# Raw weight blocks in one ring of six, and two of four weight sums made by accumulating DMAs

## The chip, the cores and the metric

The kernel runs on one core of a Trainium2 chip. The metric is the device time of one execution in microseconds; of several executions the median counts. The engines are named as in the profile: PE (matrix products; PEld its weight loads), DVE (elementwise work on two operands), ACT (activations and copies), POOL (small elementwise work, and DMAs of its own), SP (issues most of the DMAs). Each engine takes its instructions in order.

## The reference

One decoder block on x of 1024 tokens by 1024 columns, all in float32:

```python
proj = x @ w_in                     # 1024 x 7168: q | f | i | og | pool_v | gate_a | gate_b
a = HGRN2(q, f, i)                  # 8 heads, state recurrence in chunks
a = per-head RMSNorm(a) * g * sigmoid(og) @ w_a
b = per-group linear(causal_mean_w(pool_v) - pool_v) * pool_scale   # 4 groups, windows 2, 4, 8, 16
mix = (sigmoid(gate_a) * a + sigmoid(gate_b) * b) @ w_out
x = LN(alpha * x + mix)
x = LN(alpha * x + relu(x @ w_up)^2 @ w_down)      # w_up 1024 x 4096
```

## The kernel before

**Products.** Each float32 operand is split into two parts of a shorter type (`split`, L115 to L120: ACT copies the high part, L118, DVE subtracts for the low part, L119), and a product is the sum of three matmuls (`prod`, L201, L203, L204). The large products follow the Winograd form of Strassen's scheme: of an operand's four blocks, seven products instead of eight are made, from blocks and sums of blocks. On the side of the tokens the operands are a11, a12, a22 and the sums s1 to s4. They stay in SBUF, split, for a whole stage.

**A pair.** `pair` takes two column blocks of a weight, 128 columns each. Both have an upper and a lower half of 512 rows: b11 and b21 are the first column block, b12 and b22 the second. Seven operands are made from them (`t0` is b11, `b_21`, `t3`, `t2`, `t1`, `t4`, `b_22`), each split into two tiles of the ring "w" of ten, and seven products `p1` to `p7` of twelve matmuls each are added into three PSUM banks (a, c, z). ACT copies a bank (L271) where its sum so far is needed, DVE adds (L275). The four sums of weight blocks are DVE instructions: L241 (`w_diff`, twice), L284 and L289, or L291 and L292 in a "twin" pair. In a pair that is no twin, t3 and t2 are made together and then p6 and p7 run; then t1 and t4, then p5 and p4. In a twin (the pairs of w_a, and the first two of w_up) the order is p7, p4, p6, p5, each with its operand.

**Raw weights.** A pair has two raw tiles, one for each half of the rows; each holds two blocks of 256 KB. `raw_tile` is a ring of two, so one pair fills it. SP issues the loads: L217 where the two column blocks are neighbours (one DMA of 512 KB for each tile), L223 where they aren't (four of 256 KB). The sums go to a ring "t" of two tiles.

**Stages in order.** The values (v = x @ their part of w_in), the heads, the gates and pools, the product with w_a, that with w_out and the first norm, the up products with w_up, the down products with w_down and the last norm. In the heads stage the pairs of the next head (`head_inputs`), the output gates (every second head) and the pools stand beside the recurrence `hgrn` of the current head, whose small factors are made by POOL (L819 to L838). After the last head come the gates, the pool products and the sums of o (`EXTRAS[7, 1]`, `o_sums` L608 to L613). The up stage runs sixteen pairs, the first three interleaved, the others one after the other.

**Order of work.** The program is written stage by stage, and a planner orders the instructions of each engine by priorities and its own model of their times: an instruction whose operands are ready passes one that still has to wait. The order is then fixed. DMAs are issued by an engine in that order too, and an issue that waits for a buffer holds what is behind it on the same engine.

Of the kernel before, what the change touches and what calls it, by code (L numbers as in the profile page):

```python
# [43 lines left out]
def tile_hybrid_block(  # L44
# [126 lines left out]

    def first_tokens(name, *tags):
        for kp in range(CH):
            ps, _ = transposed(r[:CH], HALF if name == "a12" else 0, kp, tags[kp % len(tags)])
            in_parts(name, kp, ps)
            A.copy(xt[name == "a12"][kp], ps)

    def second_tokens(name, *tags):
        a11, a12, s = xt
        turned = []  # L180
        for kp in range(CH):
            if name in ("s3", "a22"):
                ps, done = transposed(r[CH:], HALF if name == "a22" else 0, kp, tags[kp % len(tags)])
                turned.append(done)
            if name == "s3":
                V.tensor_sub(s[kp], a11[kp], ps)
            elif name == "s1":
                V.tensor_add(a11[kp], s[kp], a11[kp])
            elif name == "s4":
                V.tensor_sub(a12[kp], a12[kp], s[kp])  # L190
            in_parts(name, kp, dict(s3=s, s2=s, s1=a11, s4=a12)[name][kp] if name != "a22" else ps)
            if name == "a22":
                V.tensor_sub(s[kp], ps, s[kp])
        return turned
# [11 lines left out]
    def raw_tile():  # L206
        return wq.tile([P, CH, 2, P], F32, tag="raw", name=nm("raw"), bufs=2)

    def w_blocks(src, c1, c2, tile_of=raw_tile):

        raw = tile_of(), tile_of()

        def load(*which):
            for kh in range(2):
                rows_of = src[kh * HALF : (kh + 1) * HALF, :].rearrange("(k p) c -> p k c", p=P)
                if c2 == c1 + P and len(which) == 2:
                    done = nc.sync.dma_start(  # L217
                        out=raw[kh].rearrange("p k n c -> p k (n c)"), in_=rows_of[:, :, c1 : c1 + 2 * P]
                    )
                else:  # L220
                    for n in which:
                        c = (c1, c2)[n]
                        done = nc.sync.dma_start(out=raw[kh][:, :, n], in_=rows_of[:, :, c : c + P])  # L223
            return done

        return raw, load

    def loaded_blocks(*args):
        raw, load = w_blocks(*args)
        load(0, 1)  # L230
        return raw
# [6 lines left out]

    def w_diff(a, b):
        t = wq.tile([P, CH, P], F32, tag="t", name=nm("t"), bufs=2)  # L240
        V.tensor_sub(t, a, b)  # L241
        return t
# [20 lines left out]
    def pair(raw, rooms, takes, pz_tag="pj", twin=False, pc_tag="pj"):  # L263


        b11, b12, b21, b22 = raw if len(raw) == 4 else (raw[kh][:, :, n] for kh in range(2) for n in range(2))
        c, ps = {}, {}
# [10 lines left out]
        def t3():  # L278
            c["t"] = w_diff(b22, b12)
            return w_part(c["t"])  # L280

        def t2():
            if not twin:
                V.tensor_add(c["t"], c["t"], b11)  # L284
            return w_part(c["t"])

        def t4():
            if not twin:
                V.tensor_sub(c["t"], b21, c["t"])  # L289
                return w_part(c["t"])  # L290
            V.tensor_add(c["t"], c["t"], b11)  # L291
            V.tensor_sub(b21, b21, c["t"])  # L292
            return w_part(b21)

        def t1():
            return w_part(w_diff(b12, b11))
# [17 lines left out]
        def p6(w):  # L314
            prod(ps["a"], w, "s2", False)
            with tc.high_priority(PRIO):
                c[21] = copied(rooms[1], ps["a"])
                if twin:
                    takes[2](added(c[21], ps["z"]))

        def p4(w):
            prod(ps["z"], w, "a22", False)
            if not twin:
                with tc.high_priority(PRIO):
                    takes[2](added(c[21], ps["z"]))
# [17 lines left out]
        def b_22():  # L343
            return w_part(b22)

        return (
            ((t0,), ((t0, p1),)),
            ((b_21,), ((b_21, p2),)),
            *(
                (((t3,), ((t3, p7),)), ((t4,), ((t4, p4),)), ((t2,), ((t2, p6),)), ((t1,), ((t1, p5),)))  # L350
                if twin
                else (((t3, t2), ((t2, p6), (t3, p7))), ((t1, t4), ((t1, p5), (t4, p4))))
            ),
            ((b_22,), ((b_22, p3),)),
# [47 lines left out]
    with tc.tile_pool(name="xr", bufs=8, side="right", reuse_waits="tile") as xr:  # L402
# [42 lines left out]
        def raw_tile_rows():  # L445
            return [raw_tile().rearrange("p k n c -> p (k n c)").rearrange("p (k c) -> p k c", c=HALF) for _ in range(2)]
# [78 lines left out]
        def take_p5(c, ps):  # L525
            V.tensor_add(c22[c], c22[c], ps)
            put(1, 1, c, c22[c])

        def take_p3(c, ps):
            t = c_soon()  # L530
            A.copy(t, ps)
            put(0, 1, c, t)
# [9 lines left out]
        with behind_parts("a12"):  # L542
            for k in range(CH):
                V.tensor_sub(b22[k], b22[k], b12[k])
            w = parts(b22)
# [3 lines left out]
        with behind_parts("s3"):  # L549
            for k in range(CH):  # L550
                V.tensor_add(b22[k], b22[k], b11[k])
                V.tensor_sub(b21[k], b21[k], b22[k])
            w = parts(b21)
# [7 lines left out]
        with tc.issue_after(taken["a22", 1]):  # L561
            for k in range(CH):
                V.tensor_sub(b12[k], b12[k], b11[k])
# [21 lines left out]
    def raw_rows(src, k2, cc):  # L585

        raw = raw_tile().rearrange("p k n c -> p (k n c)").rearrange("p (k c) -> p k c", c=HALF)
        rows_of = src[k2 * P : (k2 + 2) * P, cc * HALF : (cc + 1) * HALF].rearrange("(k p) c -> p k c", p=P)
        nc.sync.dma_start(out=raw, in_=rows_of)
# [15 lines left out]
    def o_sums(kp, tile_of=c_tile):  # L605

        a11, a21, a12, a22 = (loaded(od[k][u], tile_of) for k, u in ((kp, 0), (kp, 1), (kp + CH, 0), (kp + CH, 1)))
        V.tensor_add(a22, a21, a22)  # L608
        V.tensor_sub(a21, a11, a21)
        V.tensor_sub(a11, a22, a11)  # L610
        V.tensor_sub(a12, a12, a11)
# [6 lines left out]
    with tc.tile_pool(name="tmp", bufs=1, side="right", reuse_waits="tile") as tmp:  # L618
# [24 lines left out]
        def head_inputs(h, behind=()):  # L643
# [6 lines left out]
            def take_f(u):  # L650
                def take(src):
                    t = fs[u] = fs[u] or tt("f")
                    A.activation(t, src, AF.Sigmoid)
# [3 lines left out]
            def take_q(u):  # L657
# [7 lines left out]
                loaded_blocks(w_in, h * P, D + h * P), (c_soon, c_late, room_f),  # L665
# [8 lines left out]
        def output_gates(h):  # L674

            def take(dst, src=False):
                def put(t):
                    s = c_late() if src else t
                    A.activation(s, t, AF.Sigmoid)
# [4 lines left out]
                loaded_blocks(w_in, 3 * D + h * P, 3 * D + (h + 1) * P), (c_soon, c_late, c_late),  # L684
                (take(ogd[h][0]), take(ogd[h + 1][0], True), take(ogd[h][1]), take(ogd[h + 1][1])),
            ))

        def gates(j):
# [3 lines left out]
            def take(dst, src=None, more=None):  # L692
                def put(t):
                    s = (tt("v") if spare else c_late()) if src else t
                    more_of = loaded(more, lambda: tt("v")) if more is not None else None
                    A.activation(s, t, AF.Sigmoid)
# [7 lines left out]
                loaded_blocks(w_in, 5 * D + j * P, 6 * D + j * P), rooms,  # L704
                (take(gad[j][0]), take(gbd[j][0], True, more[0]), take(gad[j][1]), take(gbd[j][1], False, more[1])),
            ))

        def pool_products(g):
# [6 lines left out]
            raw = raw_tile().rearrange("p k n c -> p (k n c)")[:, : 2 * 2 * P].rearrange("p (k c) -> p k c", c=2 * P)  # L715
# [16 lines left out]
        def pooled(g):  # L732
# [3 lines left out]
            def mean(c, u):  # L736

                for lo in (QUARTER, 0):
# [8 lines left out]
                    if u == 0 and lo == 0:  # L747
                        n += win - 1
                        V.tensor_mul(cur[:, HALO:n], cur[:, HALO:n], inv_n[:, : win - 1])
                        V.tensor_sub(pv[:, HALO:n], cur[:, HALO:n], pv[:, HALO:n])  # L750
                    V.scalar_tensor_tensor(pv[:, n:], cur[:, n:], 1.0 / win, pv[:, n:], ALU.mult, ALU.subtract)
# [11 lines left out]
            def first(c, i):  # L763
                G.memset(c[:, :HALO], 0.0)
                mean(c, 0)
                put(c, i, 0)

            def second(c, i):
                mean(c, 1)
# [12 lines left out]
            def take_12(ps):  # L782
# [7 lines left out]
                loaded_blocks(w_in, 4 * D + j * P, 4 * D + (j + 1) * P),  # L790
# [154 lines left out]
        nxt = head_inputs(0, (None, None, "p6", None, None))  # L945
# [40 lines left out]
        def gated(j, u, park):  # L986

            def take(src):
                t = loaded(gad[j][u], mg_tile("ga", 12))
                V.tensor_mul(t, t, src)  # L990
# [10 lines left out]
        def a_pair(p):  # L1001
            raw = loaded_blocks(w_a, 2 * p * P, (2 * p + 1) * P, raw_tile if p % 2 else mg_raw)
            room = mg_tile("room", 4)
            takes = [gated(2 * p + i, u, p < 2) for u in range(2) for i in range(2)]
            return pair(raw, (c_tile, room, room), takes, "hg", True)
# [76 lines left out]
    with tc.tile_pool(name="wo", bufs=1, side="right", reuse_waits="tile") as mp:  # L1082
        st1 = [None] * 8
        g1, b1 = ln_params(lambda: f(act_tile()).rearrange("p a b -> p (a b)"), ln1_g, ln1_b)
        for k2 in range(0, KT, 2):
            raw = raw_rows(w_out, k2, 1)
            for k in range(2):
                n = len(wo)
                out_row(raw[:, k], (
# [46 lines left out]
    with tc.tile_pool(name="up", bufs=1, side="right", reuse_waits="tile") as up:  # L1136
# [10 lines left out]
        def relu2(t, src):  # L1147
            A.activation(t, src, AF.Relu)
# [3 lines left out]
        def units(i, raw):  # L1152
# [5 lines left out]
            def take(n):  # L1158
                def take(src):
                    h[n] = relu2(c_tile() if n == 1 else src, src)  # L1160
# [20 lines left out]
            return pair(raw, (c_tile,) * 3, (take(0), last, take(2), take(3)), "hg", i < 2, "tr" if i == 2 else "pj")  # L1181

        def up_blocks(i):
            return w_blocks(w_up, i * 2 * P, i * 2 * P + P, up_raw_tile if i % 2 else raw_tile)

        blocks = [up_blocks(i) for i in range(2)]
        for _, load in blocks:
            load(0, 1)
        pairs = [units(i, raw) for i, (raw, _) in enumerate(blocks)]
# [21 lines left out]
        for i in range(3, NP):  # L1211
            raw, load = up_blocks(i)
            w_load = load(0, 1)
            if i == NP - 2:
                for part in down_rows(0, ws0):
                    part(w_load)
# [185 lines left out]
```

## Time and profile before

| | |
|---|---|
| median of 3 runs | 1461.98 us (1461.56 to 1463.47) |
| the profiled execution | 1460.19 us |
| its span, first to last instruction | 1458.5 us |
| granted clock, mean | 0.996 |
| PE, DVE, ACT, POOL busy | 98%, 78%, 52%, 4% |
| moved by DMA | 226.82 MB, 156 GB/s over the span |

The profile is one execution; times in it are counted from its first instruction. An engine is busy while an instruction of its own runs. Matmuls overlap, so the number of matmuls in a stretch says more of PE's pace than the duration of one. "A <- B" in a list of waits means that A stood idle until B released it.

### The profile page before, as it was taken

How to read it: one execution, taken by the hardware profiler on the slowest of the kernel's cores; microseconds unless marked ns; L12 is line 12 of the kernel's file. 1: busy time of each engine (PE TensorE's matmuls, PEld its weight loads, DVE VectorE, ACT ScalarE, POOL GpSimd, SP SyncE). 2: the span in 40 equal slices, each digit the busy share in tenths (PEclk: the TensorE clock that was granted, in tenths of full speed). 3: DMA queues.
4: the chain of work that ended last, by engine and by line, in shares of the span. 5: the costliest groups of instructions: out<-in, count | busy, mean ns of one | idle time of the engine just before them, and what ended most of it. 6: DMA issues, size and time to landing. Idle time of an engine off the chain costs nothing.

```text
span 1458.5 us, 20662 instructions
## 1 busy us (share of the span) xinstructions
PE 1436.4 (98%) x7377; PEld 1187.9 (81%) x7377; DVE 1141.6 (78%) x1838; ACT 758.3 (52%) x1383; POOL 58.6 (4%) x244
## 2 busy tenths in 40 slices
PE   8999999999999998999999999999999999999997
PEld 7888888888888886788888878888888888888886
DVE  5967989899898885768985597666666787777977
ACT  5445565666656655556542376555555443333535
POOL 0001001001000010000002100000000100000000
PEclk9999999999999999999999999999999999999999
DMA  7232233323234447897672225444474874445322
GB/s 253 70 126 87 85 98 101 109 75 114 90 99 138 152 132 249 301 299 241 223 247 99 73 94 195 159 146 144 152 261 149 275 260 150 153 141 163 130 73 116
DMA packets 160615, 226.82 MB, mean 156 GB/s; under 512 B 11232, under 2 KB 84480, under 8 KB 160512
## 3 DMA queue, kind: packets, MB, share of 16 engines
q1 hardware_dynamic: 158576, 218.93, 44.7%
q0 software_dynamic: 1152, 4.19, 0.8%
q10 hardware_dynamic: 784, 2.38, 0.5%
q8 instruction: 58, 0.95, 0.3%
q14 instruction: 45, 0.37, 0.1%
HBM read 154.16 MB, written 71.30 MB: 155 GB/s over the span
## 4 chain that ended last, share of the span: by engine, by line
PE 94%; DVE 3%; DMA 1%; ACT 1%; issue 0%; SPq 0%; DVEq 0%
PE ps_pj L201 16%; PE ps_pj L203 16%; PE ps_pj L204 16%; PE ps_pj L1283 4%; PE ps_pj L1285 4%; PE ps_pj L1284 4%; PE ps_pj L106 3%; PE ps_pj L107 3%; PE ps_pj L105 2%; PE ps_tr L1285 1%; PE ps_tr L1283 1%; PE ps_tr L1284 1%; PE ps_sc L201 1%; PE ps_sc L203 1%; PE ps_sc L204 1%; PE ps_hg L203 1%
## 5 line engine op out<-in xcount | busy, mean ns | idle before, releaser
L201 PE MATMUL ps_pj<-act,w 128*128 128x512 f32 x1068 | 421.6, 395 | 0.4 <-ACT act L123 0.2
L203 PE MATMUL ps_pj<-act,w 128*128 128x512 f32 x1068 | 415.1, 390 | 0.5 <-DVE act L124 0.5
L204 PE MATMUL ps_pj<-act,w 128*128 128x512 f32 x1068 | 414.1, 390 | 0.0
L201 PEld LDWEIGHTS ps_pj<-act,w 128*128 128x128 f32 x1068 | 200.6, 188 | 42.8 <-ACT act L123 0.6
L204 PEld LDWEIGHTS ps_pj<-act,w 128*128 128x128 f32 x1068 | 200.5, 188 | 42.3
L203 PEld LDWEIGHTS ps_pj<-act,w 128*128 128x128 f32 x1068 | 200.6, 188 | 40.6 <-DVE act L124 0.9
L118 ACT CAST w<-t 128x512 fp32r<-128x512 f32 x170 | 104.7, 620 | 105.0 <-PE ps_pj L203 53.8
L118 ACT CAST w<-raw 128x512 fp32r<-128x512 f32 x143 | 88.2, 620 | 117.3 <-PE ps_pj L203 62.5
L119 DVE TENSOR_TENSOR w<-raw,w 128x512 fp32r<-128x512 f32 x143 | 99.8, 702 | 55.2 <-ACT w L118 53.9
L119 DVE TENSOR_TENSOR w<-t,w 128x512 fp32r<-128x512 f32 x170 | 115.9, 685 | 29.6 <-ACT w L118 29.4
L1245 ACT CAST act<-act 128x1024 fp32r<-128x1024 f32 x66 | 66.9, 1050 | 107.9 <-issue 35.0
L1246 DVE TENSOR_TENSOR act<-act,act 128x1024 fp32r<-128x1024 f32 x66 | 79.3, 1220 | 18.5 <-ACT act L1245 15.8
L1285 PE MATMUL ps_pj<-act,act 128*128 128x512 f32 x240 | 92.9, 389 | 0.0
L1284 PE MATMUL ps_pj<-act,act 128*128 128x512 f32 x240 | 92.9, 389 | 0.0
L1283 PE MATMUL ps_pj<-act,act 128*128 128x512 f32 x240 | 92.4, 389 | 0.0
L275 DVE TENSOR_TENSOR c<-c,ps_pj 128x512 f32<-128x512 f32 x95 | 64.5, 681 | 18.0 <-PE ps_pj L204 13.4
L271 ACT COPY c<-ps_pj 128x512 f32<-128x512 f32 x96 | 55.2, 582 | 12.8 <-PE ps_pj L204 12.8
L817 DVE RECIPROCAL tC<-tA 128x128 f32<-128x128 f32 x64 | 54.1, 904 | 0.0
L1284 PEld LDWEIGHTS ps_pj<-act,act 128*128 128x128 f32 x240 | 45.1, 188 | 9.4
L1285 PEld LDWEIGHTS ps_pj<-act,act 128*128 128x128 f32 x240 | 45.1, 188 | 9.4
L1283 PEld LDWEIGHTS ps_pj<-act,act 128*128 128x128 f32 x240 | 45.1, 188 | 9.3
L241 DVE TENSOR_TENSOR t<-raw,raw 128x512 f32<-128x512 f32 x43 | 29.6, 689 | 21.9 <-DMA raw<-in_w_in_dram 19.7
(415 smaller groups left out, 2719.8 us busy)
## 6 DMA issues: line engine op xcount, KB each, us to landing
h<-c SPq DMA_DIRECT2D x106, 256.0 KB, 2.1
act<-h SPq DMA_DIRECT2D x78, 256.0 KB, 2.9
raw<-in_w_in_dram SPq DMA_DIRECT2D x64, 256.0 KB, 3.4
draw<-in_w_down_dram SPq DMA_DIRECT2D x16, 1024.0 KB, 7.8
raw<-in_w_up_dram SPq DMA_DIRECT2D x30, 512.0 KB, 4.2
raw<-in_w_in_dram SPq DMA_DIRECT2D x18, 512.0 KB, 4.0
hf<-h SPq DMA_DIRECT2D x34, 256.0 KB, 2.9
c<-o SPq DMA_DIRECT2D x24, 256.0 KB, 3.4
```

Source lines behind the costliest of these rows:

```text
L118: A.copy(hi, src)
L119: V.tensor_sub(lo, src, f(hi))
L201: PE.matmul(ps, wh[:, k], th, start=first and k == 0, stop=False, skip_group_check=True)
L203: PE.matmul(ps, wh[:, k], tl, start=False, stop=False, skip_group_check=True)
L204: PE.matmul(ps, wl[:, k], th, start=False, stop=k == CH - 1, skip_group_check=True)
L271: A.copy(t, ps)
L275: V.tensor_add(t, t, ps)
L1245: A.copy(hi, src)
L1246: V.tensor_sub(lo, src, f(hi))
L1283: PE.matmul(ps, hh[:, w], wh, start=fresh and n == 0, stop=False, skip_group_check=True)
L1284: PE.matmul(ps, hh[:, w], wl, start=False, stop=False, skip_group_check=True)
L1285: PE.matmul(ps, hl[:, w], wh, start=False, stop=n == M - 1, skip_group_check=True)
```

## The change

- All raw blocks are tiles of their own, [128, 4, 128], in one ring of six (`block_tile`) in place of the two rings "raw" and "t". A pair uses five of them: four blocks and one for a sum. Other users of the raw ring take one to four such tiles. Pairs 1 and 3 of w_a and all pairs of w_up from the fourth on, with the first, now load single blocks of 256 KB (`loaded_blocks`); pairs 0 and 2 of w_a and the second of w_up keep wide loads in rings of their own (`wide_blocks`).
- In the heads, the output gates, the gates and the pools (`summed_blocks`), the sums b22 + b12 and b11 + b12 are made by loading one block with SP and adding the other onto it with an accumulating DMA from POOL (`accum_op=ALU.add`). DVE makes the other two sums. Elsewhere DVE makes all four.
- So that all sums of weight blocks are additions, b12 and b21 stand with the other sign in the scheme. The sums of token blocks change with them (`minus_sum`), and where a result comes out negative its sign is taken back at its use (a scale of -1 in an activation, a sign in `gated`, the other operation in the pools).
- Every pair now runs in the order t0 p1, b_21 p2, t3 p7, t4 p4, t2 p6, t1 p5, b_22 p3, each operand with its product.

```diff
+    def minus_sum(out, a, b):
+        V.scalar_tensor_tensor(out, a, -1.0, b, ALU.mult, ALU.subtract)
...
-    def raw_tile():
-        return wq.tile([P, CH, 2, P], F32, tag="raw", name=nm("raw"), bufs=2)
...
+    def block_tile(shape=(CH, P)):
+        return wq.tile([P, *shape], F32, tag="raw", name=nm("raw"), bufs=6)
+
+    def wide_block(src, kh, c, t):
+
+        rows_of = src[kh * HALF : (kh + 1) * HALF, :].rearrange("(k p) c -> p k c", p=P)
+        done = nc.sync.dma_start(out=t, in_=rows_of[:, :, c : c + t.shape[2]])
+        return t, done
+
+    def loaded_blocks(src, c1, c2, done=None):
+
+        raw = {}
+        for i in ((0, 0), (1, 0), (0, 1), "t", (1, 1)):
+            raw[i] = block_tile(), None
+            if i != "t":
+                raw[i] = wide_block(src, i[0], (c1, c2)[i[1]], raw[i][0])
+        if done is not None:
+            done.append(raw[1, 1][1])
+        return [raw[i][0] for i in ((0, 0), (0, 1), (1, 0), (1, 1), "t")]
+
+    class Summed(tuple):
+        pass
+
+    def summed_blocks(src, c1, c2):
+
+        def load(t, kh, n, onto=False):
+            rows_of = src[kh * HALF : (kh + 1) * HALF, :].rearrange("(k p) c -> p k c", p=P)
+            rows_of = rows_of[:, :, (c1, c2)[n] : (c1, c2)[n] + P]
+            if onto:
+                nc.gpsimd.dma_start(out=t, in_=rows_of, accum_op=ALU.add)
+            else:
+                nc.sync.dma_start(out=t, in_=rows_of)
+
+        b11, b21, t3, t1, b22 = (block_tile() for _ in range(5))
+        load(b11, 0, 0)
+        load(b21, 1, 0)
+        load(t3, 1, 1)
+        load(t3, 0, 1, True)
+        load(t1, 0, 0)
+        load(t1, 0, 1, True)
+        load(b22, 1, 1)
+        return Summed((b11, t1, b21, b22, t3))
...
         def t3():
-            c["t"] = w_diff(b22, b12)
+            if not summed:
+                c["t"] = block_tile() if t is None else t
+                V.tensor_add(c["t"], b22, b12)
             return w_part(c["t"])
 
+        def t4():
+            if not summed:
+                V.tensor_add(b12, b12, b11)
+            V.tensor_add(c["t"], b22, b12)
+            V.tensor_add(b21, b21, c["t"])
+            return w_part(b21)
+
         def t2():
-            if not twin:
-                V.tensor_add(c["t"], c["t"], b11)
             return w_part(c["t"])
...
         def t1():
-            return w_part(w_diff(b12, b11))
+            return w_part(b12)
...
+        return tuple(
+            ((operand,), ((operand, product),))
+            for operand, product in ((t0, p1), (b_21, p2), (t3, p7), (t4, p4), (t2, p6), (t1, p5), (b_22, p3))
         )
...
             run(pair(
-                loaded_blocks(w_in, h * P, D + h * P), (c_soon, c_late, room_f),
+                summed_blocks(w_in, h * P, D + h * P), (c_soon, c_late, room_f),
...
-        def relu2(t, src):
-            A.activation(t, src, AF.Relu)
+        def relu2(t, src, n):
+            A.activation(t, src, AF.Relu, scale=-1.0 if n % 2 else 1.0)
...
-            raw, load = up_blocks(i)
-            w_load = load(0, 1)
+            done = []
+            raw = loaded_blocks(w_up, i * 2 * P, i * 2 * P + P, done)
```

151 lines of the change are left out of this document (57 added, 94 removed).

## The prediction

> **What bounds the kernel now.** I read the page's parts 1 and 4 first, then the stretches, the waits, and the timeline where the one gap stands.
>
> ```profile
> span 1458.5 us, 20662 instructions
> PE 1436.4 (98%) x7377; PEld 1187.9 (81%) x7377; DVE 1141.6 (78%) x1838; ACT 758.3 (52%) x1383; POOL 58.6 (4%) x244
> PE 94%; DVE 3%; DMA 1%; ACT 1%; issue 0%; SPq 0%; DVEq 0%
> ```
> ```profile
> 300.00:350.00 50.00, 50.00 (x348) 41.72 (x347) 48.96 (x100) 33.24 (x76) 4.50 (x26) 1.00 0.30 95
> 550.00:600.00 50.00, 43.25 (x252) 34.83 (x252) 28.76 (x52) 24.34 (x57) 0.00 (x0) 0.93 0.77 254
> 600.00:650.00 50.00, 50.00 (x221) 40.96 (x220) 31.91 (x50) 25.79 (x44) 0.00 (x0) 1.00 0.95 315
> 1000.00:1050.00 50.00, 50.00 (x222) 41.44 (x221) 29.25 (x45) 26.72 (x45) 0.00 (x0) 1.00 0.45 148
> ```
>
> A stretch shows its length, then busy PE, PEld, DVE, ACT, POOL, the granted clock, the DMA share and GB/s. TensorE carries 94% of the chain and works 50.00 of 50 us in the heads (300:350), the gates (600:650) and the up stage (1000:1050). There 222 matmuls fill 50 us: 0.225 us each, so a product of one weight block (12 matmuls) takes 2.70 us. The change leaves every matmul in place, so it can win only where TensorE stands still, above all in 550:600, where 6.75 us are missing; DMA is busy there at 0.77, and at 0.95 right after.
>
> **The gap at 577 us.** PE's waits, then the rows of all engines that lead to the longest, in order of time:
>
> ```profile
> PE ps_pj L105 <- ACT w L118: 4.7, 1, 4.7
> PE ps_hg L915 <- DVE st L883: 1.2, 1, 1.2
> PE ps_pj L106 <- DVE w L119: 0.8, 1, 0.8
> ```
> ```profile
> 561.72 1.89 SPq L223 DMA_DIRECT2D raw<-in_w_in_dram  x2
> 568.57 0.69 DVE L241 TENSOR_TENSOR t<-raw,raw 128x512 f32<-128x512 f32 x1 [2.93 <-DMA raw<-in_w_in_dram]
> 569.78 0.17 DVE L925 RECIPROCAL ss<-ss 128x4 f32<-128x4 f32 x1
> 569.99 1.14 ACT L928 ACTIVATE tH<-ps_hg,ss 128x128 f32<-128x128 f32 x4 [2.10 <-DVE ss L925]
> 572.44 0.63 ACT L696 ACTIVATE c<-c 128x512 f32<-128x512 f32 x1
> 573.10 0.34 SPq L699 DMA_DIRECT2D gb<-c  x1
> 577.18 0.48 SPq L594 DMA_DIRECT2D og<-po  x1
> 582.18 0.62 ACT L118 CAST w<-og 128x512 fp32r<-128x512 f32 x1 [2.75 <-DMA og<-po]
> 582.85 1.22 PE L105 MATMUL ps_pj<-w,q 128*128 128x512 f32 x2 [4.66 <-ACT w L118]
> 583.87 0.63 PE L106 MATMUL ps_pj<-w,q 128*128 128x512 f32 x1
> 584.29 0.63 PE L107 MATMUL ps_pj<-w,f 128*128 128x512 f32 x1
> 580.00:590.00 10.00, 7.11 (x20) 4.82 (x20) 4.10 (x7) 6.54 (x13) 0.00 (x0) 0.66 0.66 222
> ```
>
> The two weight loads issued from 561.72 on are all there at 568.57. DVE, which takes its work in order, stands 2.93 us before the difference L241 that needs them. Behind it stands the small reciprocal L925, ACT waits for that, so the sigmoid L696 and its store at 573.10 come late, SP gets to the load og<-po only at 577.18, its data are there at 582.18, and PE has stood 4.66 us. After this gap the clock is 0.66 and matmuls follow each other 0.42 us apart (583.87 to 584.29), not 0.225: for about a dozen matmuls that costs another 2.3 us (an estimate, 12 x 0.195). So the gap is worth 9.1 us in all (6.75 + 2.3).
>
> **Part by part.**
>
> *DVE's work.* Of the four weight sums of a pair of blocks in the heads, pools and gates (24 pairs: 8 + 4 head pairs, 4 pools, 8 gates) two go to DMAs: 48 additions.
>
> ```profile
> L284 DVE TENSOR_TENSOR t<-t,raw 128x512 f32<-128x512 f32 x37 | 25.5, 688 | 0.7
> ```
>
> 48 x 0.688 = 33 us of DVE go. In 300:350 DVE is busy 48.96 of 50, but PE is at 50.00: beside PE this is worth nothing, directly. The sign changes (one DVE form for another, a scale in an activation) are as many instructions as before: nothing.
>
> *When weights arrive.* Before, the two raw tiles of a pair hold two blocks each and come free only after the fourth sum and the last split:
>
> ```profile
> SPq L223 <- DVE t L284: 56.0, 9, 11.6
> ACT w L118 <- PE ps_pj L203: 123.5, 107, 4.3
> ```
>
> SP holds loads until DVE's L284, and the splits run ahead until the ring of ten split tiles is full (ACT waits 107 times for PE to release one), so operands are made at PE's pace, one per 2.70 us. By the order of the operands a raw tile is refilled two to three operands before its next use (5.4 to 8.1 us). In the ring of six, with five blocks per pair, the third block of the next pair takes the place of the second of this one, freed by the fourth operand and wanted as third operand of the next: six operands, 16.2 us; the fourth has six too, the last five. So the loads come 8 to 11 us earlier against need, and the DVE row that starts the gap no longer exists: its sum is a DMA's. I take the 2.93 us off the 4.66, leaving 1.7 us. For the clock, the stretch before the long wait:
>
> ```profile
> 570.00:580.00 10.00, 6.98 (x44) 5.75 (x42) 5.09 (x9) 5.68 (x17) 0.00 (x0) 1.00 0.57 182
> ```
>
> It holds the wait of 1.2 us and still has 1.00; 1.7 us is nearer to that than to 4.66, so I take all of the 2.3 us off (none, if the clock falls all the same).
>
> The Trainium skill (TensorE: Matmul & The Clock Gate, section "Part 1: The HAM clock gate") lets the clock fall to half only after an idle window of about 3.4 us. By it, half of the 2.93 us would do to keep the clock, and the gap would give -1.5 - 2.3 = -3.8 us; by the rows, silent between 1.2 and 4.66 us, such a half might give only -1.5.
>
> Gap: -2.93 - 2.3 = -5.2 us.
>
> *The accumulating DMAs.* Each summed pair issues seven loads of 256 KB instead of 1 MB in all: +0.75 MB, for three of them inside the busiest stretch. No row shows an accumulating DMA. Nearest rows: the plain 256 KB loads in 110:550 and in 550:690, all queue-1 traffic of 550:690, and POOL's own loads of 512 KB (landing, then issue):
>
> ```profile
> raw<-in_w_in_dram SPq DMA_DIRECT2D x48, 256.0 KB, 3.3
> raw<-in_w_in_dram SPq DMA_DIRECT2D x12, 256.0 KB, 5.5
> q1 hardware_dynamic: 27239, 38.09, 82.2%
> act<-x POOLq DMA_DIRECT2D x7, 512.0 KB, 6.7
> L1293 POOL DMA_DIRECT2D act<-x x7 | 3.9, 559 | 331.0 <-DVE c L275 324.2 <-PE ps_pj L204 6.3
> ```
>
> A sum takes load + issue + accumulation. Quiet: 3.3 + 0.6 + 3.3 = 7.2 us at the least, and 3.3 + 2.2 + 6.7 = 12.2 us if issue grows fourfold with four times the rows and the accumulation lands like 512 KB. Both are under 16.2 us. Busy: 5.5 + 0.6 + 5.5 = 11.6 us, up to 5.5 + 2.2 + 11.2 = 18.9 us (6.7 scaled by 5.5/3.3). I take 12 to 13, nearer the row of equal size, so 0 us; the end is the second rival. DMA share of 550:690: 82.2% x (38.09 + 9 x 0.26)/38.09 = 87%, or 91% if an accumulation counts twice.
>
> *The queues passed.* POOL now also holds two DMAs per pair, each waiting for its base load; behind it stand the small products of the head recurrence (L819 to L838), for which DVE waits. Bound: nothing, or the 2.9 us that follow.
>
> ```profile
> DVE t L241 <- DMA raw<-in_w_in_dram: 13.3, 10, 2.9
> PE ps_tr L870 <- DVE tC L865: 0.2, 1, 0.2
> ```
>
> These are DVE's and PE's waits of 100:560. DVE stood ten times, up to 2.9 us, for a late load, and PE lost 0.2 us in all. That is the cover: delays of this size are absorbed, and DVE gains 33 us of slack. I take 0. SP issues more (five loads for four or two), at 0.4 us each, in a queue that mostly waits: 0.
>
> *The order of products.* The old order p6, p7, p5, p4, p3 becomes p7, p4, p6, p5, p3, and p4 adds onto the bank that p7 has just filled and ACT must copy first:
>
> ```profile
> 1000.17 0.39 PE L204 MATMUL ps_hg<-act,w 128*128 128x512 f32 x1
> 1000.89 0.58 ACT L271 COPY c<-ps_hg 128x512 f32<-128x512 f32 x1
> 299.88 0.39 PE L204 MATMUL ps_pj<-act,w 128*128 128x512 f32 x1
> 300.20 0.31 PE L887 MATMUL sc<-tF,tD 128*32 128x32 f32 x10
> 303.60 0.50 PE L201 MATMUL ps_pj<-act,w 128*128 128x512 f32 x1
> ```
>
> The next product could start at 1000.40; the copy ends at 1001.47: 1.07 us if nothing stands between, at three places of a pair (p7-p4, p6-p5, p5-p3). The last three rows show the planner putting work of another kind (L887, earlier in the program) between products when it becomes ready; p6, whose operand is made five ahead, can stand between p7 and p4. I take 0; uncovered, 13 up pairs x 3 x 1.07 = 42 us.
>
> Sum against the profiled execution's 1460.19 us: 1460.19 - 5.2 = 1455.0. The median of the runs lies 1.8 us above it: 1456.8 us.
>
> **Rivals.** About 0.2% (2.9 us) is what a measurement of this kernel can tell from no change.
>
> *The gap stays* (0.13). The planner's order around 577 us comes out new, and another late row of SP's queue, as og<-po, makes the same wait. For it: DMA is still at 0.8 there. Between -2.9 and +2.9: 1462 us.
>
> *Late sums in the gates, slower* (0.27). In 550:690 three summed gate pairs run at a DMA share near 0.9. If a sum takes more than the 16.2 us of its lead, ACT stands before its split and, once five operands of lead are eaten, PE too. At the upper bound of 18.9 us: 2.7 us per pair and sum, two sums, three pairs: +16 us; from one sum per pair +8 us, with the gap kept: 1470 us, bounds 1465 to 1478. Against it: the stage's PE had 50.00 at a share of 0.95. The page "DMA: Bandwidth & Descriptors" of the Trainium skill, section "Bandwidth", prices a DMA at 2.0 us plus bytes over 436e3 and asks for transfers of 1 MiB; by it 256 KB takes 2.6 us (an estimate), where the rows show 3.3 and 5.5. By the page this rival would have no chance; the rows decide.
>
> *Products in program order, slower* (0.09). If the planner leaves a third of the 39 places open: +14 us, 1476 us; all, 1504.
>
> *POOL holds the recurrence, slower* (0.07). The small products are late by more than DVE's slack in each of 16 half heads, by 1 us each: +16, 1478 us.
>
> **How the numbers follow.** The forecast's chance is 0.44: the chain of the gap is read row by row, but the new order is not. Its own range is 1453 (the whole 9.1 us gone) to 1459 (only the 2.93). Faster 0.44, same 0.13, slower 0.27 + 0.09 + 0.07 = 0.43. The range reaches to 1452 below and 1475 above; outside lie the upper ends of the last three rivals.
>
> **What would show it.** Right: no DVE row waiting for raw in the heads, 48 fewer DVE additions, PE's longest wait near 580 us under 2 us, no clock below 1 there, PE at 50.00 in 300:350 and 1000:1050. Wrong: ACT's L118 waiting for accumulated blocks with PE behind it in 550:690; PE waiting for L271 in the up stage; POOL's L819 late and DVE behind it. More than 1 us of PE waits per pair in heads or up stage would overturn the forecast.

## The result, and the profile after

The changed kernel is slower: 1473.01 us median of four runs (1470.55 to 1473.54) beside 1462.6 us for the kernel before on the same chip, a ratio of 1.0065 with a 95% interval of 1.0052 to 1.0078 (the quotient of the medians, 1.0071, lies in it). Its profiled execution took 1470.55 us with a span of 1468.8 us, 10.3 us above the span of before. The forecast was 1456.8 us and faster. From here on "after" is the changed kernel. The medians below leave out one execution each of e1, e2 and e4 that ran at a clock of 0.85 or less and took 1606 to 2407 us.

The page after, parts 1 and 4, then the stretches that the prediction named, with the one behind the gates, 650:700, where the clock fell:

```profile
span 1468.8 us, 20993 instructions
PE 1441.7 (98%) x7377; PEld 1189.2 (81%) x7377; DVE 1111.4 (76%) x1790; ACT 758.6 (52%) x1383; POOL 118.9 (8%) x292
PE 88%; DMA 6%; DVE 4%; ACT 1%; issue 1%; SPq 1%; DVEq 0%; POOL 0%; ACTq 0%; POOLq 0%
```
```profile
300.00:350.00 50.00, 50.00 (x343) 41.37 (x342) 46.81 (x96) 32.49 (x75) 9.76 (x29) 1.00 0.54 132
550.00:600.00 50.00, 43.42 (x257) 33.91 (x256) 30.87 (x57) 26.88 (x65) 2.61 (x2) 0.97 0.80 247
600.00:650.00 50.00, 47.57 (x209) 38.70 (x207) 28.02 (x45) 23.69 (x42) 5.12 (x4) 0.99 1.09 340
650.00:700.00 50.00, 49.80 (x213) 40.50 (x212) 40.40 (x65) 29.63 (x55) 0.00 (x0) 0.97 0.75 251
1000.00:1050.00 50.00, 50.00 (x222) 41.39 (x222) 31.43 (x49) 29.34 (x50) 0.00 (x0) 1.00 0.47 158
```

DVE lost 48 instructions and 30 us, and the heads and the up stage stand at 50.00 of 50 as before. The chain has 6% DMA instead of 1%. The stretch 600:650, full before (50.00, DMA share 0.95), misses 2.43 us of PE at a DMA share of 1.09, and 650:700 runs at a clock of 0.97, where before has 1.00.

Where the 10 us arose can be read from the matmuls themselves, because every kernel here makes the same 7377. The table gives how much later than in before the n-th 128x512 matmul starts, in us, with the time of before in the head. At these four places every kernel has also made the same number of other matmuls (89 at the first, 1457 at the other three), so the columns can be compared even where the order of products differs. The last column stands past the gates; what follows it adds a constant 0.8 us at about 885 us in the kernels with the ring. Each row is one execution, and 21 executions of before alone spread from 1460.22 to 1464.62 us, so a difference of 2 us between two rows may be chance.

| kernel | n = 400 (108 us) | 2200 (610) | 2400 (656) | 2600 (702) |
|---|---|---|---|---|
| after | +1.75 | +3.39 | +7.69 | +8.83 |
| e1_dve_sums | +3.78 | +0.17 | +5.50 | +6.46 |
| e2_gates_dve | +4.49 | +5.82 | +5.62 | +6.99 |
| e3_plain_onto | +2.00 | +3.50 | +4.66 | +5.84 |
| e4_gates_only | +5.36 | +7.56 | +12.25 | +13.86 |
| e5_old_order | +3.17 | -1.05 | +6.77 | +7.26 |
| e7_start_wide | +0.22 | +1.98 | +4.99 | +6.75 |
| e6_ring_only | +0.27 | +6.66 | +10.93 | +12.57 |
| e8_heads_only | +0.05 | +4.54 | +4.77 | +6.68 |
| n9_before_new_order | +0.23 | +0.47 | +0.67 | +3.29 |
| n10_dve_wide_start | 0.00 | -1.77 | +4.56 | +5.60 |
| n12_before_four_loads | +3.40 | +5.54 | +6.71 | +6.58 |
| n13_o_sums_later | -0.28 | +1.86 | +12.21 | +13.93 |

After loses 1.75 us in the first 108 us, 1.6 us up to 610 us, 4.3 us from 610 to 656 us and 1.1 us up to 702 us. The heads have no part in it: from 110 to 540 us PE waits 0.2 us in all, as in before. The list of PE's waits of after shows the same places:

```profile
PE ps_pj L105 <- ACT w L118: 2.8, 2, 2.4
PE ps_pj L105 <- ACT q L118: 2.4, 1, 2.4
PE ps_pj L486 <- ACT act L123: 1.9, 1, 1.9
PE ps_pj L204 <- ACT w L118: 1.6, 2, 1.0
PE ps_pj L204 <- ACT c L291: 1.1, 1, 1.1
```

The columns are the sum, the number of waits and the longest. Four of these rows have no row of their size in before; only the first is the gap that the prediction was about, and it shrank from 4.7 to 2.4 us. The timeline of after gives their places, PE's rows alone:

```profile
547.17 0.50 PE L204 MATMUL ps_pj<-act,w 128*128 128x512 f32 x1 [1.01 <-ACT w L118]
556.11 0.50 PE L204 MATMUL ps_pj<-act,w 128*128 128x512 f32 x1 [1.13 <-ACT c L291]
586.88 0.73 PE L105 MATMUL ps_pj<-w,q 128*128 128x512 f32 x2 [2.42 <-ACT w L118]
648.07 0.50 PE L105 MATMUL ps_pj<-w,q 128*128 128x512 f32 x1 [2.43 <-ACT q L118]
```

The first one begins with a load of another stage. From the timeline of ACT and SP in after:

```profile
537.87 0.37 SPq L725 DMA_DIRECT2D raw<-in_w_pool_dram  x1
542.72 0.62 ACT L118 CAST q<-raw 128x512 fp32r<-128x512 f32 x1 [4.67 <-DMA raw<-in_w_pool_dram]
546.52 0.60 ACT L118 CAST w<-raw 128x512 fp32r<-128x512 f32 x1
```

ACT stood 4.67 us for a load that SP issued at 537.87 us, and the split for PE, behind it, came at 546.52. The pool weights use the ring of six too.

### The profile page after: what moved, and what is told of

Same layout as the page of the kernel before. It is cut to its first block, busy times and chain, and to the rows that moved or that the text cites. A ratio compares the mean times of both kernels' runs of the same rounds, so it can differ in the third digit from the quotient of the medians.

```text
span 1468.8 us, 20993 instructions
## 1 busy us (share of the span) xinstructions
PE 1441.7 (98%) x7377; PEld 1189.2 (81%) x7377; DVE 1111.4 (76%) x1790; ACT 758.6 (52%) x1383; POOL 118.9 (8%) x292
## 3 DMA queue, kind: packets, MB, share of 16 engines
q10 hardware_dynamic: 784, 2.38, 0.5%
## 4 chain that ended last, share of the span: by engine, by line
PE 88%; DMA 6%; DVE 4%; ACT 1%; issue 1%; SPq 1%; DVEq 0%; POOL 0%; ACTq 0%; POOLq 0%
PE ps_pj L204 15%; PE ps_pj L207 15%; PE ps_pj L206 15%; PE ps_pj L1291 4%; PE ps_pj L1292 4%; PE ps_pj L1293 4%; DMA raw<-in_w_in_dram 3%; PE ps_pj L105 2%; PE ps_pj L106 2%; PE ps_pj L107 2%; PE ps_tr L1291 1%; PE ps_tr L1292 1%; PE ps_tr L1293 1%; PE ps_hg L207 1%; PE ps_sc L207 1%; PE ps_sc L206 1%
## 5 line engine op out<-in xcount | busy, mean ns | idle before, releaser
L118 ACT CAST w<-raw 128x512 fp32r<-128x512 f32 x311 | 191.6, 622 | 242.8 <-PE ps_pj L206 150.4
L119 DVE TENSOR_TENSOR w<-raw,w 128x512 fp32r<-128x512 f32 x311 | 211.2, 687 | 104.1 <-ACT w L118 101.8
L295 DVE TENSOR_TENSOR c<-c,ps_pj 128x512 f32<-128x512 f32 x95 | 64.7, 682 | 35.0 <-PE ps_pj L207 31.9
L243 POOL DMA_DIRECT2D raw<-in_w_in_dram x48 | 62.3, 1364 | 326.1 <-DMA raw<-in_w_in_dram 111.8
L291 ACT COPY c<-ps_pj 128x512 f32<-128x512 f32 x96 | 55.7, 582 | 15.3 <-PE ps_pj L207 9.8
L1162 ACT ACTIVATE c<-c 128x512 f32<-128x512 f32 x61 | 38.7, 634 | 1.5
L1161 ACT ACTIVATE c<-c 128x512 f32<-128x512 f32 x46 | 29.1, 633 | 15.8 <-DVE c L295 15.8
```

The costliest lines, as they stand in the source:

```text
L118: A.copy(hi, src)
L119: V.tensor_sub(lo, src, f(hi))
L243: nc.gpsimd.dma_start(out=t, in_=rows_of, accum_op=ALU.add)
L295: V.tensor_add(t, t, ps)
```

## The experiments

Four questions: do the accumulating DMAs cost the time, and by POOL's queue or by the DMA engines; does the start; does the order of products; and does the ring do so by itself. The ratios are those to the kernel before on the same chip, with their 95% intervals.

### Whose sums, and by whom: e1, e2, e4

e1 takes every accumulating DMA out, e2 only those of the gates, e4 all but those of the gates.

```diff
 e1: at all four calls; e2: at the gates (5 * D + j * P) alone; e4: at the other three
-    summed_blocks(w_in, ...
+    loaded_blocks(w_in, ...
```

> All 24 summed pairs take their sums from DVE again (four plain loads of 256 KB, none onto another); the ring of six, the signs and the order of products stay as in the changed kernel. Theory A (the accumulating DMAs are the loss: an estimate from queue 0 in 110:550 is 18.3% of 440 us over 38 of them, 2.1 us of all 16 DMA engines each): back to 1461 to 1464 us, and the DMA share of 600:650 falls from 1.09 to about 0.95. Theory B (the ring, the order of products and the new plan are the loss, whoever sums): 1470 to 1474 us.

> Only the eight gate pairs go back to DVE sums; heads, output gates and pools keep the accumulating DMAs. Theory A: of the loss, 5.4 us lie between 610 and 702 us of the trace, where the gates meet the pool products; these go, the rest stays: 1466 to 1468 us. Theory B: 1470 to 1474 us.

> The reverse of the second: only the eight gate pairs take sums by accumulating DMAs, heads, output gates and pools sum on DVE. Theory A with the loss where DMA is full: 1467 to 1470 us. Theory C (POOL's queue in the heads): 1462 to 1464 us. Theory B: 1470 to 1474 us.

| kernel | accumulating in heads, output gates, pools | in the gates | median | ratio |
|---|---|---|---|---|
| after | yes | yes | 1473.01 | 1.0065 [1.0052, 1.0078] |
| e2_gates_dve | yes | no | 1467.55 | 1.0033 [1.0019, 1.0046] |
| e4_gates_only | no | yes | 1472.74 | 1.0075 [1.0062, 1.0089] |
| e1_dve_sums | no | no | 1467.53 | 1.0037 [1.0023, 1.0050] |

The sums of the gates cost 5.2 us (e4 over e1), and 5.5 us (after over e2); those of the other stages nothing either way (e2 over e1 0.0 us, after over e4 +0.3 us). From 110 to 550 us POOL issues 38 of them among the recurrence's small products, and PE hardly waits there; so its queue isn't what costs. Half of the loss goes with the gates' sums, and half doesn't: without any accumulating DMA the kernel is still 0.37% slower.

The price is the same in both pairs of kernels, the place is not. From the 2200th to the 2600th matmul after loses 5.4 us and e2 1.2; e4 and e1 lose 6.3 us each, and what e4 loses more lies ahead of 610 us. Each of these edits also changes the planner's order on PE, from about 383 us on, so the two pairs alone don't tell the DMAs from the plan.

PE's waits of 590 to 660 us, from the list of waits of e2, then of e4 (there up to 670 us):

```profile
PE ps_pj L105 <- ACT w L118: 2.7, 2, 2.2
PE ps_pj L204 <- ACT w L118: 0.3, 1, 0.3
```
```profile
PE ps_pj L105 <- ACT w L118: 3.1, 2, 2.7
PE ps_pj L105 <- ACT q L118: 2.7, 1, 2.7
PE ps_pj L106 <- DVE w L119: 1.3, 2, 1.0
```

The wait for q, after's 2.43 us at 648.07, is there in e4 and gone in e2. Taken alone it is no sign of accumulating DMAs: n10 (below), which has none, waits for q too, as its list of 540 to 700 us shows:

```profile
PE ps_pj L105 <- ACT q L118: 2.2, 1, 2.2
```

### The adding or the issue: e3

e3 leaves POOL's loads where they are, with the same instructions in the same order on every engine, and takes the addition off them.

```diff
-                nc.gpsimd.dma_start(out=t, in_=rows_of, accum_op=ALU.add)
+                nc.gpsimd.dma_start(out=t, in_=rows_of)
```

> The second load of a summed block is still issued by POOL, at the same place, with the same wait and the same bytes, but it overwrites instead of adding (the sums are left out, so the output is not the reference's). The order on every engine is that of the changed kernel. Theory A, if the price is the accumulation itself: the transfer takes about 0.9 us of the DMA engines instead of 2.1, the gap at 648 us closes: 1464 to 1467 us. Theory A, if the price is 0.75 MB more per pair: 1470 or more. Theory C (POOL's queue holds the recurrence): no change, 1471 to 1474 us.

Measured: 1469.87 us, ratio 1.0056 [1.0042, 1.0070]. By the medians that is 3.1 us below after, by the ratios 1.3 us, and the two intervals overlap, so the reading rests on the rows. The DMA queues of 110 to 550 us (packets, MB, share of 16 engines) and the landings, of after and of e3; then the stretch 600:650 of e3 and of e1:

```profile
q1 hardware_dynamic: 69582, 51.24, 38.2%
q0 software_dynamic: 20024, 9.95, 18.3%
raw<-in_w_in_dram SPq DMA_DIRECT2D x95, 256.0 KB, 4.0
raw<-in_w_in_dram POOLq DMA_DIRECT2D x38, 256.0 KB, 6.5
```
```profile
q1 hardware_dynamic: 70267, 51.61, 37.9%
q0 software_dynamic: 3040, 9.96, 8.0%
raw<-in_w_in_dram POOLq DMA_DIRECT2D x38, 256.0 KB, 4.5
```
```profile
600.00:650.00 50.00, 49.37 (x216) 40.14 (x215) 29.86 (x48) 24.36 (x42) 2.99 (x4) 1.00 1.02 348
600.00:650.00 50.00, 47.07 (x198) 37.55 (x197) 30.61 (x49) 21.92 (x39) 0.00 (x0) 0.97 0.95 317
```

An accumulating DMA of 256 KB takes 18.3% x 440 / 38 = 2.1 us of all 16 engines, in 527 packets; the same bytes without the addition 8.0% x 440 / 38 = 0.93 us in 80 packets, and a load of SP about 0.86 us (38.2% x 440 us for 51.24 MB). So the addition costs the engines 1.2 us for each block; with it the packets are also smaller (some 0.5 KB each instead of 3.3), and no run tells the one from the other. The Trainium skill (Collectives: The Full Stack, section "The bandwidth ceiling: the fold count and why AG ≠ RS ≠ AR") says of the reduction in a collective that its addition needs two source reads where a copy needs one. That agrees in direction; the factor here is 2.3. In 600:650, where the engines are full, e3 misses 0.63 us of PE where after misses 2.43, and the clock stays at 1.00. The loss from the 2200th to the 2400th matmul is 1.2 us instead of 4.3, and up to the 2600th 2.3 instead of 5.4 (e7, which has after's order there and its accumulating DMAs, loses 4.8). The order is the same, so another plan is no rival here, though each row is one execution. But a lower share alone doesn't keep PE busy: e1, with no accumulating DMA and a share of 0.95, has another plan and misses 2.93 us in the same stretch, by waits for L119 (1.7 us) and L295 (1.2 us). The rows of SP around the place, of after and then of e3, show where a full set of engines is felt:

```profile
644.57 3.65 SPq L603 DMA_DIRECT2D c<-o  x3
```
```profile
643.71 2.69 SPq L603 DMA_DIRECT2D c<-o  x3
```

The same three issues take 3.65 us instead of 2.69. The split that PE waits for came at 647.40 us in after, after ACT had stood 5.31 us, and at 645.60 in e3, after 4.33 us. The trace names a different store as its releaser in each, so which transfer held it isn't settled. In e1 and n10 ACT stands 3.80 and 4.27 us before this split too. e3 also shows that not all of the gates' 5 us is the adding; the rest goes with having the loads on POOL or with the plan that they bring, which no run here separates.

### The start: e7, n12, n10

The values stage loads its block b22 through the raw ring: before two tiles of 512 KB, after four of 256 KB. e7 gives after its two wide loads back (in the tiles of another ring), n10 does so in e1, and n12 puts four loads into before. On every engine each has another order than the kernel it is made of in the first 110 us alone.

```diff
 e7 and n10
-        blocks = b11, b22, b21, b12 = wide_rows(), raw_tile_rows(), act_rows(), act_rows()
+        blocks = b11, b22, b21, b12 = wide_rows(), act_rows(), act_rows(), act_rows()
 n12, in before
-            return [raw_tile()... for _ in range(2)]
+            ts = [raw_tile()... for _ in range(2)]
+            return [t[:, k : k + 1] for t in ts for k in range(2)]
```

> The changed kernel with one edit at its start: the block b22 of the values stage goes to two tiles of 512 KB (two loads) as before, not to four of the ring of six (four loads). In the order of instructions ACT then casts the first token block before the third weight row again, as in the kernel before; in the changed kernel three casts for rows that are still on their way stand ahead of it. Theory F (this order is the start's loss, 1.3 to 1.8 us of the profile by 108 us, up to 5 in the other runs where the clock falls too): PE's wait of 1.9 us for L123 at 12 us is gone, and the time is 1.5 to 4 us less: 1468 to 1471 us. Theory B (any new plan costs that much): 1471 to 1474 us.

> The kernel before with one edit: b22 of the values stage comes by four loads of 256 KB instead of two of 512 KB. The order of ACT then has the casts of four weight rows ahead of the first token block, as in the changed kernel; behind the start no engine's order differs. Theory F: 1.5 to 4 us more, 1464 to 1467 us, all of it before 65 us, with PE's wait of about 2 us for L123. Theory B: no difference, 1461 to 1463 us.

> The first experiment (no accumulating DMAs, ring of six, new order) with the wide start of the seventh. Theory F: 1467.6 less 1.5 to 3.5 us, so 1464 to 1466 us; what is left against the kernel before, 1.5 to 3.5 us, would be the ring's and the order's. If the start does not add up with it: 1467 us.

Measured: n12 1467.34 us, ratio 1.0035 [1.0023, 1.0048]: 5 us from cutting two loads in two. e7 1468.93 us, 1.0048 [1.0035, 1.0062], and n10 1465.57 us, 1.0022 [1.0012, 1.0031]: 2 to 4 us come back when they are joined, though here the intervals overlap those of after and e1, so that n12 is the firm one of the three. By the 400th matmul e7 and n10 are where before is (+0.22 and 0.00 us, after and e1 +1.75 and +3.78). The timeline of ACT at the start, of before and then of after:

```profile
7.04 0.62 ACT L118 CAST w<-b 128x512 fp32r<-128x512 f32 x1 [1.86 <-DMA b<-in_w_in_dram]
7.56 0.58 ACT L123 CAST act<-ps_tr 128x512 fp32r<-128x512 f32 x1
10.59 0.62 ACT L118 CAST w<-b 128x512 fp32r<-128x512 f32 x1 [2.45 <-DMA b<-in_w_in_dram]
```
```profile
7.00 0.62 ACT L118 CAST w<-b 128x512 fp32r<-128x512 f32 x1 [2.04 <-DMA b<-in_w_in_dram]
10.34 1.14 ACT L118 CAST w<-b 128x512 fp32r<-128x512 f32 x2 [2.73 <-DMA b<-in_w_in_dram]
11.50 1.05 ACT L123 CAST act<-ps_tr 128x512 fp32r<-128x512 f32 x2
```

Before, the first token block (L123) goes at 7.56 us and the third weight row waits at 10.59. After, ACT takes the third and fourth weight rows first and stands 2.73 us for their load with the token block behind it. That load is one of b, another block than b22: what changed is the planner's order of ACT. n12 has the same order and the same wait, here from PE's waits of n12 and its first stretch:

```profile
PE ps_pj L478 <- ACT act L123: 2.0, 1, 2.0
0.00:50.00 50.00, 44.75 (x218) 37.39 (x218) 30.97 (x57) 24.45 (x44) 2.06 (x28) 0.97 0.53 190
```

By the 400th matmul n12 is 3.4 us late. The wait is the smaller part of it: before stands 1.9 us at the start too, for a load of x, and from 0 to 110 us PE is idle for 5.40 us in n12 and 4.71 in before. The clock of 10:20 is 0.83 in n12 and 1.00 in before, which takes another 1.7 us; the last 1.0 us is not located. The other 3 us of n12 arise later, up to 656 us, although there every engine has before's order: the same plan lost more when it came to the seam later.

### The order of products: e5, n9

n9 gives before the order of after in every pair; e5 gives after the order of before in the pairs that were no twins.

```diff
 n9, in before's pair
+        twin = True
...
-        nxt = head_inputs(0, (None, None, "p6", None, None))
+        nxt = head_inputs(0, (None, None, "p6", None, None, None, None))
```

> The changed kernel with all its DMA sums and its ring, but with the old order of products (p6, p7, p5, p4) and of operands (t3, t2, then t1, t4) in every pair that had it before. Theory D (a part of the loss that stays without accumulating DMAs, 5.4 us in the first experiment, comes from the new order, where PE waits for ACT's copy L291 of the bank it has just filled, 1 to 2 us at a time between 545 and 617 us): 2 to 4 us less than the changed kernel, 1468 to 1470 us, and no PE wait for L291 of a c tile. Theory E (the order doesn't matter): 1471 to 1474 us.

> The kernel before with one edit: every pair runs in the new order (p7, p4, p6, p5, each operand with its product); rings, loads, sums and signs stay. Theory D (order costs by PE waiting for the copy of the bank just filled): 2 to 5 us more, 1464 to 1467 us, with PE waiting for L271. Theory G (the order is harmless in itself; what is lost between 545 and 700 us hangs on which late DMA each plan lets DVE or ACT stand before, ahead of the last head's recurrence): either sign, 1458 to 1468 us, all of the difference between 540 and 700 us.

Measured: n9 1464.80 us, ratio 1.0016 [1.0007, 1.0025], so +2.3 us; e5 1469.14 us, 1.0043 [1.0031, 1.0056], some 3 to 4 us below after, with intervals that just touch. n9's loss lies between the 2400th and the 2600th matmul (0.67 to 3.29 us); the row of PE there:

```profile
658.78 0.50 PE L204 MATMUL ps_pj<-act,w 128*128 128x512 f32 x1 [1.61 <-DVE w L119]
```

It is a wait for DVE's split, not for ACT's copy of a bank, which the expectation named. In the up stage (1000:1050) n9 has PE at 50.00 of 50 like before and after. In this trace the order costs at the seam between the heads and the product with w_a, where pairs of several kinds meet, and nowhere else.

### What is left of the change: e8, e6, n13

e8 is e2 with the old order and the wide start; e6 is e1 with both; n13 is e6 with one part of the sums of o, ("o_sums", 2), behind a pair of gates.

```diff
 n13, in the list of what follows the last head
-            ("gates", 4), ("o_sums", 2), ("pool_products", 0), ("gates", 5), ("pool_products", 1),
+            ("gates", 4), ("pool_products", 0), ("gates", 5), ("o_sums", 2), ("pool_products", 1),
```

> As the ring alone, but with accumulating DMAs in heads, output gates and pools, where 2.1 us of the DMA engines per sum meet a share of 0.3. If POOL's queue and DMA's share in the heads cost nothing, as the first, second and fourth experiment suggest (0.3 to 0.5 us apart): the time of the ring alone, 1460 to 1464 us, and perhaps below, since DVE has 22 us less to do; if they cost: 2 us or more above it.

> All sums on DVE, the old order of products, the wide start: of the change there remain the ring of six single blocks and the signs. If accumulation in the gates, the new order and the start make up the loss: 1460 to 1464 us, within 0.2% of the kernel before. If the ring or a new plan as such costs: 1466 to 1469 us, as in the first experiment.

> The kernel of the ring alone (1470.3 us) with one edit: the third sum of o (o_sums 2) stands behind gates 5 in the program, not ahead of the first pool product. In that kernel DVE stood 3.3 us for the load c<-o of this sum at 578 us, ahead of the small reciprocal that the last head needs, and PE stood 5.8 us. Theory G: that wait goes and the time falls by 3 to 8 us, 1462 to 1467 us. If the ring itself starves the gates: 1469 us or more.

Measured: e8 1468.18 us, ratio 1.0033 [1.0021, 1.0044]; e6 1470.33 us, 1.0058 [1.0045, 1.0070]; n13 1476.28 us, 1.0096 [1.0082, 1.0110]. e6 has no accumulating DMA, the old order and the old start, and should have been the fastest. At the start it is where before is (+0.27 us); then it loses 6.4 us up to the 2200th matmul and 5.9 us up to the 2600th. From the timelines of DVE and PE in e6, and its clock behind the gap:

```profile
578.80 0.69 DVE L633 TENSOR_TENSOR c<-c,c 128x512 f32<-128x512 f32 x1 [3.27 <-DMA c<-o]
580.13 0.17 DVE L953 RECIPROCAL ss<-ss 128x4 f32<-128x4 f32 x1
580.76 0.47 PE L959 MATMUL ps_tr<-ident,tH 128*128 128x128 f32 x1 [5.77 <-ACT tH L956]
580.00:600.00 20.00, 15.88 (x58) 12.84 (x59) 9.83 (x19) 8.32 (x26) 0.00 (x0) 0.63 0.56 186
```

This is the chain of before's gap with another first member: DVE stands for a load (c, for the sums of o, instead of a weight), the small reciprocal stands behind it, ACT and PE behind that. I supposed that moving the sums of o away would mend it. n13 refutes that, with 6 us more: the wait for tH falls from 5.8 to 3.5 us, and a new one of 4.5 us appears, as PE's waits of n13 show:

```profile
PE ps_pj L204 <- ACT c L291: 4.5, 1, 4.5
PE ps_tr L959 <- ACT tH L956: 3.5, 1, 3.5
PE ps_pj L106 <- DVE w L119: 3.0, 2, 1.6
```

So the parts don't add: order, start and accumulating DMAs each cost 2 to 5 us when undone or added alone, yet with all three undone 8 us are left. In the table the loss from the 400th to the 2600th matmul is anything from 2.5 us (e2) to 14.2 us (n13). The planner's order at the seam matters: n13 moves one sum and takes 6 us more than e6. It is not all: behind 110 us n10 has the order of e1 and loses 5.6 us where e1 loses 2.7, and n12 has that of before and loses 3.2 (single executions). What rule makes one plan good and another bad there stays open.

None of the versions beats before; the nearest are n9 and n10.

## Why the prediction was wrong

**The sign.** Three costs were taken at nothing and are not nothing.

- *The accumulating DMAs* were the step that failed. "I take 12 to 13 ... so 0 us" asked only whether a sum arrives within its lead of 16.2 us. By the medians it does: in 590:650 the base load lands in 5.4 us, the issue takes 1.3, and the accumulation lands in 8.6, 15.3 us together; and from 550 to 690 us no split of after waits for a raw block of w_in. What was not asked is what it takes from the others at a share of 0.95. The share of 550:690 is 0.87 in after, as forecast, but that spreads over 140 us what falls within 50: there it is 1.09. The price was 5 us by the two pairs of kernels and 1 to 3 us by e3, where only the addition is missing. The place of the second rival was right for after; its price (+8 to +16 us) was above that, and its mechanism, ACT before a late sum, did not appear, since the longest wait stands before a split (q) that has no accumulated operand.
- *The start* was not costed at all. That other users of the ring get smaller tiles stood in the change, and the number of loads was read as a matter of SP's queue. It changed the order at the start, ACT's above all: 2 to 5 us.
- *The order of products* was taken at 0 with 42 us if uncovered. It is +2.3 us (n9). For the up stage the reason was right, PE is at 50.00 there; but the seam was not looked at, and the cost is there.

**The gain.** The gap did shrink, by 2.2 us (4.66 to 2.42) where 2.93 were forecast. The wait of DVE for raw blocks is gone. What is left is mostly not the load og<-po, for which ACT now stands 0.51 us instead of 2.75, but ACT's place in the last head: it takes the rows of L935 first, for which it has to wait, and then the split that PE needs.

```profile
584.56 0.28 ACT L935 ACTIVATE tH<-ps_hg 128x128 f32<-128x128 f32 x1 [3.39 <-PE ps_hg L930]
586.21 0.62 ACT L118 CAST w<-og 128x512 fp32r<-128x512 f32 x1 [0.51 <-DMA og<-po]
```

The clock came back only in part: the half clock lasts 3.4 us in after (0.89 in 580:590 and 0.94 in 590:600) and 6.8 us in before (0.66 in 580:590), where the forecast took all of it off. "I take all of the 2.3 us off" needed a remainder of 1.7 us. And what the gap gave was spent ahead of it, 2.1 us of it on the new waits at 547 and 556 us: from the 400th to the 2200th matmul, across the heads and the gap, after loses 1.6 us against before, where a gain of 5.2 was forecast. The rival "the gap stays" had this mechanism, in a milder form.

**What held.** DVE's 33 us were worth nothing (30 us went, and e1, which gives them back to DVE, is not slower). POOL's queue cost nothing: e2 and e1 are equal, and PE's waits of 110 to 540 us are 0.2 us. Issue (1.30 us median) and landing (6.5 us, busy 8.6) lie within the bounds given. No wait for L291 appears in the up stage. Of the signs named for "wrong" in 550:690, an ACT split late with PE behind it did show the loss, though not before an accumulated block.

**The bound on the page's price.** The rows were to decide between the 2.6 us worked out from the Trainium skill and the rows' 3.3 to 5.5 us for 256 KB. They side with the rows: 4.0 us in 110:550, and 5.4 in 590:650. The fit itself stands in another section of that page of the Trainium skill (DMA: Bandwidth & Descriptors, section "Anatomy of one DMA — SWDGE (gpsimd) path") and is for DMAs that GpSimd issues. The nearest rows to it are POOL's: 256 KB landed in 4.5 us without the addition (e3) and in 6.5 with it, both above 2.6.

## What to carry to other kernels

Price a transfer in a full stretch by the time it takes of the DMA engines, not by whether its own data come in time: here an accumulating DMA took what two plain loads take (2.1 us beside 0.9). Look for the stretch with the highest share and count over its length, not over the stage's. Where a planner fixes the order, cutting a load in two is a change of the schedule, and its cost is found by doing that part alone on the kernel before. Where another plan alone moves the time by several us, the effect of one part is read from an edit that leaves every engine's order as it is, as e3 does.

## What the runs showed of the hardware

The length of a wait alone doesn't tell whether the clock falls. After's wait of 2.43 us, up to 648.07 us, is followed by the half clock from 649.29 to 652.70 us. In e7 PE waits 2.38 us up to 646.60 us, for the same split, and the clock stays at 1.00. Stretches of 3.41 us, of after and then of e7:

```profile
645.88:649.29 3.41, 1.22 (x5) 0.86 (x5) 0.72 (x2) 1.89 (x4) 0.00 (x0) 1.00 1.02 376
649.29:652.70 3.41, 3.41 (x9) 2.49 (x9) 2.61 (x5) 1.29 (x3) 0.00 (x0) 0.50 0.85 290
```
```profile
641.78:645.19 3.41, 2.44 (x11) 1.69 (x9) 0.67 (x2) 0.00 (x0) 0.00 (x0) 1.00 1.09 385
645.19:648.61 3.42, 1.91 (x7) 1.20 (x8) 1.51 (x3) 2.68 (x6) 0.00 (x0) 1.00 1.02 378
```

In all fourteen traces each half clock ahead of the last 20 us lasts 3.41 us or a multiple of it, so e7's trace can be cut into the same stretches, counted from its own half clock at 587.16 us. After's wait fell almost whole into one of them, which had PE idle for 2.19 of 3.41 us; e7's fell across two, idle for 0.97 and 1.51. The traces cut up in this way from 20 to 1440 us have 21 stretches at full clock with 1.8 us or more of idle time; 20 of them are followed by the half clock (one of e2, with 1.9 us idle, is not), and none of those with less is. The Trainium skill (TensorE: Matmul & The Clock Gate, section "Part 1: The HAM clock gate") states an idle window of about 3.4 us that runs freely. The length agrees; that the whole window has to be idle does not. The prediction's working by that rule, under which half of the 2.93 us would have kept the clock, did not hold either: 2.2 us were saved and the clock still fell.

An accumulating DMA of 256 KB in 512-byte rows holds POOL for 1.30 us, the same load without the addition for 0.75 us (medians of after and e3).
